# A Mamba-2 scan pipelined by one chunk, with three of its products on GpSimd

## The chip, the cores and the metric

One core of a Trainium2 chip runs the kernel. The metric is the device time of one execution in microseconds (us); less is better. TensorE (PE in the profile) multiplies matrices, VectorE (DVE) and ScalarE (ACT) work element by element, GpSimd (POOL) too, and SyncE (SP) issues most DMAs. Every engine works through its own queue in order.

## The reference

Two layers over 2048 tokens of width 1024, in float32: a Mamba-2 mixer, then multi-head latent attention, and a last norm. The change lies in the mixer's scan, which the reference computes in chunks:

```
def step(state, inp):
    x_c, dt_c, B_c, C_c = inp
    cum = jnp.cumsum(dt_c * A_g, axis=1)
    seg = cum[:, :, None] - cum[:, None, :]
    L = jnp.exp(jnp.where(causal, seg, -jnp.inf))
    CB = jnp.einsum('btgn,bsgn->btsg', C_c, B_c)
    y_intra = jnp.einsum('btsg,btsgh,bsgh,bsghp->btghp', CB, L, dt_c, x_c)
    y_inter = jnp.einsum('btgn,bghpn,btgh->btghp', C_c, state, jnp.exp(cum))
    w_end = jnp.exp(cum[:, -1:] - cum) * dt_c
    new_state = state * jnp.exp(cum[:, -1])[..., None, None] + \
        jnp.einsum('bsgn,bsgh,bsghp->bghpn', B_c, w_end, x_c)
    return new_state, y_intra + y_inter
```

There are 32 heads of width 64 in 4 groups; each group shares B and C of width 128. Around the scan stand an input projection (z, xBC and dt), a convolution of width 4 over xBC, a gate SiLU(z), a norm and an output projection.

## The kernel before

**Items.** `mamba` goes through 16 items: four blocks of 512 tokens (b), in each the four groups (g). An item's scan (`ssd`) works on four chunks of 128 tokens (c), so there are 64 chunks in all.

**What lies beside the scan.** `ssd` is a generator of 20 steps, five for each chunk. `mamba` runs other generators, the `parts`, and takes scan steps from `ssd` at even distances between their steps. The parts of item n are the output projection of item n-1 (`outp`, 8 steps), and for item n+1 the projection to xBC (`xbc`, 16 steps: a sweep for B and C, one for x) and to z (`zgate`, 8 steps). For items up to 4 the order is outp, xbc, zgate; after that xbc comes first. At every third group the next block's normalised x (`prep16`) and its time steps (`steps`) come last. So TensorE gets big products of 512 columns with the scan's small ones between them. The framework's scheduler makes each engine's queue from this order and the priorities; at run time the queues are in order.

**Big products.** A sweep fills up to four PSUM banks ("mm", four in all), three matmuls for each product (`mm3`, L403 to L405). A bank is emptied by `evacuate`: for xBC, GpSimd copies three halo columns into a tile `craw` (three buffers; L1055), ScalarE copies the bank behind them (L1056), GpSimd saves the new halo (L1057), ScalarE makes the first tap of the convolution (L1060), VectorE the other three (cacc, L1062) and after a Tanh the last product (L1065). For z it is one Tanh and one VectorE operation (sz, L1092), for the output one VectorE operation (hs, L1121).

**A chunk of the scan**, in its five steps (small results go to the PSUM tag "tr", four banks):

1. The cumulated log decays of eight heads are fetched by one DMA, broadcast to 128 partitions, into a tile "big" of 128x1024 (two buffers, L1225). TensorE transposes B and multiplies B with C; B and C are split into halves (high and low part) for products of three matmuls. ScalarE makes the decays: eight Relu with a bias (L1237) and one Exp (L1238). VectorE multiplies them by the masked CB (L1239).
2. TensorE transposes x (L1244). VectorE makes Xd, x times dt (L1247), and y, x times D (L1250). ScalarE makes Xw, x times wend, in eight operations of 64 columns (L1253); wend holds dt.
3. Xw is split into halves Xp: ScalarE copies the high one (L1208), GpSimd subtracts (L1209). Sixteen small matmul pairs of the decays and Xd (L1260) give the chunk's own part, which VectorE adds to y (L1261). From the second chunk on C times the state (halves Sp) is added, scaled by ecum (L1266, L1267).
4. B times Xp gives the state's increment (`late3`, L410 to L412, the low half of Xp last). VectorE multiplies the state by its decay (L1277) and adds (L1278); the new state is split into halves Sp (one buffer; ScalarE and GpSimd).
5. y is multiplied by the gate (L1283), scaled, split and transposed, for `outp` of the next item.

`steps` computes dt, its cumulated sums and exponentials for a block; its work tile is a "big" buffer. `out_power` finds a scale for the output weights once, at item 4.

## Time and profile before

| | |
|---|---|
| time, median of 3 runs (lowest to highest) | 2924.01 us (2920.55 to 2924.09) |
| the profiled execution | 2919.59 us; span of its instructions 2917.8 us |
| granted TensorE clock, mean | 0.993 |
| busy, share of the span | PE 2802.7 us (96%), DVE 2189.3 (75%), ACT 1854.4 (64%), POOL 985.2 (34%) |
| DMA | 507.56 MB, mean 174 GB/s |

The span is the time from the first to the last instruction. A row of a stage view gives for each engine the busy time and the number of instructions; a row of waits gives who waited for whom, the total in us, how many times and the longest; a row of a group gives line, engine, operation, output and inputs with their shapes, the count, the busy time and mean ns of one, and the idle time before them with what ended it. Busy times of TensorE are the union of pipelined matmuls, so short waits between them do not show as idle. L numbers are lines of the kernel before.

### The profile page before, as it was taken

The page shows a single profiled execution, that of the slowest core. Times are in us where ns is not written, and L with a number is a line of the kernel's source. Part 1 is how long each engine was busy: PE and PEld are TensorE (multiplying, and loading weights), DVE is VectorE, ACT ScalarE, POOL GpSimd, SP SyncE. Part 2 cuts the span into 40 slices and gives each one's busy share as a digit, 9 for nine tenths or more (in the row PEclk, how much of TensorE's full clock was granted, in tenths as well). Part 3 has the DMA queues.
Part 4 walks back from the last instruction along what each step waited for, and adds up shares of the span by engine and source line. Part 5 has one row for each costly group of instructions (what it writes and reads, how often), then busy time and mean ns, then how long its engine had stood idle before and what let it go on. Part 6 is the DMA issues. An engine that isn't in the chain of part 4 may idle for free.

```text
span 2917.8 us, 48835 instructions
## 1 busy us (share of the span) xinstructions
PE 2802.7 (96%) x16349; PEld 1648.5 (56%) x16349; DVE 2189.3 (75%) x4757; ACT 1854.4 (64%) x4731; POOL 985.2 (34%) x1200
## 2 busy tenths in 40 slices
PE   7999999998999999999999999999999999999898
PEld 6787755444444444444455455454555555555587
DVE  6778888888877777788776654544888898889476
ACT  7888777666666555666555343432888888888322
POOL 1211112212111221122111212222888888888400
PEclk9999999999999999999999999999999999999899
DMA  5343356665657544476544765556899999999884
GB/s 187 90 120 96 97 167 209 190 186 175 186 157 241 172 127 145 121 223 189 150 140 114 240 200 193 175 171 207 165 183 182 188 187 182 182 188 197 220 265 154
DMA packets 602144, 507.56 MB, mean 174 GB/s; under 512 B 413954, under 2 KB 455938, under 8 KB 601892
## 3 DMA queue, kind: packets, MB, share of 16 engines
q1 hardware_dynamic: 590020, 466.03, 61.3%
q0 software_dynamic: 11872, 38.41, 3.7%
q8 instruction: 128, 2.10, 0.3%
q14 instruction: 124, 1.02, 0.1%
HBM read 303.37 MB, written 104.47 MB: 140 GB/s over the span
## 4 chain that ended last, share of the span: by engine, by line
PE 64%; DVE 14%; ACT 7%; DMA 7%; issue 5%; POOL 2%; SPq 1%; ACTq 0%; POOLq 0%; DVEq 0%
PE mm L403 11%; PE mm L405 11%; PE mm L404 11%; PE tr L403 5%; PE tr L405 5%; PE tr L404 5%; PE mm L1758 4%; DVE cacc L1062 3%; DMA big<-cumT 2%; PE tr L1758 2%; PE mm L1731 2%; DMA wraw<-in_ssm_w_in_dram 2%; PE tr L1731 2%; PE tr L1260 2%; ACT big L1237 1%
## 5 line engine op out<-in xcount | busy, mean ns | idle before, releaser
L1723 POOL TENSOR_TENSOR HL<-Pr,HL 128x512 f16<-128x512 f32 x320 | 370.0, 1156 | 25.6
L403 PE MATMUL mm<-xT,wsp 128*128 128x512 f16 (+1 forms) x800 | 308.4, 385 | 7.4 <-DVE sz L1092 5.3
L404 PE MATMUL mm<-xT,wsp 128*128 128x512 f16 (+1 forms) x800 | 306.1, 383 | 0.0
L405 PE MATMUL mm<-xT,wsp 128*128 128x512 f16 (+1 forms) x800 | 305.2, 383 | 0.6 <-DVE wsp L434 0.5
L1209 POOL TENSOR_TENSOR Xp<-Xw,Xp 128x512 fp32r<-128x512 f32 x64 | 87.2, 1363 | 563.1 <-ACT Xp L1208 536.5
L403 PE MATMUL mm<-wsp,xT 128*128 128x512 f16 (+2 forms) x640 | 233.6, 366 | 1.9 <-ACT craw L1056 1.3
L404 PE MATMUL mm<-wsp,xT 128*128 128x512 f16 (+2 forms) x640 | 232.9, 364 | 1.0 <-DVE wsp L442 1.0
L1717 ACT ACTIVATE Pr<-tr,nm 128x512 f32<-128x512 f32 (+3 forms) x332 | 206.2, 626 | 41.8 <-DVE nm L1712 40.1
L405 PE MATMUL mm<-wsp,xT 128*128 128x512 f16 (+2 forms) x640 | 232.5, 364 | 0.0
L1062 DVE SCALAR_TENSOR_TENSOR cacc<-craw,pack,cacc 128x512 f32<-128x512 f32 x288 | 220.8, 785 | 11.9 <-ACT cacc L1060 10.2
L1722 POOL CAST HL<-Pr 128x512 f16<-128x512 f32 x320 | 195.0, 609 | 91.2 <-ACT Pr L1717 88.7
L1717 ACT ACTIVATE Pr<-mm,nm 128x512 f32<-128x512 f32 (+3 forms) x308 | 191.9, 628 | 44.5 <-DVE nm L1712 38.7
L1706 DVE TENSOR_REDUCE mx<-tr 128x1 f32<-128x512 f32 (+3 forms) x332 | 195.6, 602 | 28.3 <-PE tr L1682 25.9
L403 PE MATMUL mm<-wsp,yT 128*128 128x512 f16 (+1 forms) x512 | 199.4, 389 | 13.3 <-DVE hs L1121 7.2
L1237 ACT ACTIVATE big<-big,d_cum 128x128 f32<-128x128 f32 x512 | 169.8, 391 | 55.4 <-DMA big<-cumT 54.8
L1706 DVE TENSOR_REDUCE mx<-mm 128x1 f32<-128x512 f32 (+3 forms) x308 | 182.1, 604 | 27.6 <-PE mm L1682 20.6
L404 PE MATMUL mm<-wsp,yT 128*128 128x512 f16 (+1 forms) x512 | 197.7, 386 | 0.5 <-DVE wsp L442 0.5
L405 PE MATMUL mm<-wsp,yT 128*128 128x512 f16 (+1 forms) x512 | 197.4, 386 | 0.0
L405 PEld LDWEIGHTS <-xT 128*128 128x128 f16 (+1 forms) x1280 | 124.5, 97 | 117.2 <-issue 2.6
L403 PEld LDWEIGHTS <-xT 128*128 128x128 f16 (+1 forms) x1280 | 125.0, 98 | 106.1 <-issue 14.4
L1253 ACT ACTIVATE Xw<-tr,d_wend 128x64 f32<-128x64 f32 x512 | 111.7, 327 | 111.7 <-DVE y L1250 99.4
L404 PEld LDWEIGHTS <-xT 128*128 128x128 f16 (+1 forms) x1280 | 125.6, 98 | 96.1 <-issue 6.8
(504 smaller groups left out, 7562.3 us busy)
## 6 DMA issues: line engine op xcount, KB each, us to landing
wsp<-w_d SPq DMA_DIRECT2D x68, 512.0 KB, 4.0
wraw<-in_ssm_w_in_dram SPq DMA_DIRECT2D x128, 256.0 KB, 3.4
big<-cumT SPq DMA_DIRECT2D x64, 512.0 KB, 4.2
wraw<-in_ssm_w_out_dram SPq DMA_DIRECT2D x64, 256.0 KB, 3.3
w_d<-wsp SPq DMA_DIRECT2D x32, 512.0 KB, 3.5
wsp<-wo_d SPq DMA_DIRECT2D x32, 512.0 KB, 4.4
st<-w_d SPq DMA_DIRECT2D x56, 256.0 KB, 2.9
wsp<-wu_d SPq DMA_DIRECT2D x28, 512.0 KB, 3.8
```

The costliest lines, as they stand in the source:

```text
L403: mm(out, l_hi, r_hi, start=start, stop=False)
L404: mm(out, l_hi, r_lo, start=False, stop=False)
L405: mm(out, l_lo, r_hi, start=False, stop=stop)
L1062: nc.vector.scalar_tensor_tensor(acc, raw[:, k:k + TB], wk[k], acc, ALU.mult, ALU.add)
L1237: act(E[:, h, :], E[:, h, :], AF.Relu, bias=ncum[:, h0 + h:h0 + h + 1])
L1253: act(Xw[:, hc], px[:, hc], AF.Copy, scale=wend[:, h0 + h:h0 + h + 1])
L1706: v.tensor_reduce(m[:, at:at + 1], s, AX.X, ALU.max, negate=True)
L1717: nc.scalar.activation(tile("Pr", n, j, c)[:, :w], bank("S", n, j, c)[:, :w], AF.Exp, bias=moves[(4 * n + j) % len(moves)], accum_out=sums ...
L1722: nc.gpsimd.tensor_copy(u[:, 0], x)
L1723: nc.gpsimd.tensor_tensor(u[:, 1], x, u[:, 0], ALU.subtract)
L1731: nc.tensor.transpose(bank("T", n, k)[:, j * P:(j + 1) * P], tile("Pr", n, j, k // 4)[:, k % 4 * P:(k % 4 + 1) * P], self.ident)
L1758: nc.tensor.matmul(o, weights, half(n, k, low), start=start, stop=not left[n][at[0]])
```

## The change

The scan's chunk is cut into functions, and the first two steps of chunk c+1 run within chunk c, across the border from one item to the next as well:

- `fetch` (the DMA of the decays) for chunk c+2 stands behind the product of chunk c that frees the buffer. Before the first chunk two are fetched.
- `decays` (step 1 without the DMA) for chunk c+1 is the first step of chunk c, `inputs` (step 2, and the halves Xp) for chunk c+1 the fourth. Step 2 is now the product of the chunk alone, step 3 both C times the state and the update of the state.
- The product of decays and CB goes from VectorE to GpSimd, and so does the state's decay. Xw is made from Xd in one GpSimd operation instead of eight on ScalarE, and wend no longer holds dt.
- The work tile of `steps` is a craw buffer with four parts in place of six, dA and cT taking the places of e and q.
- `out_power` is taken behind `xbc` of its item's parts instead of ahead of it.
- The convolution's tiles are given back at the end of `ssd` instead of at its start.

The diff; the removed lines left out stand in the functions above:

```
--- before.py
+++ after.py
@@ -880,7 +880,7 @@
     def mamba(self, cp):
         nc = self.nc
         self.state = [None] * G
-        self.xn, self.xT, self.dtv, self.conv, self.sz, self.yT, self.rr, self.hs = {}, {}, {}, {}, {}, {}, {}, {}
+        self.xn, self.xT, self.dtv, self.conv, self.sz, self.yT, self.rr, self.hs, self.scan, self.fetched = ({} for _ in range(10))
         items = [(b, g) for b in range(NB) for g in range(G)]
         self.load_x(0, self.a["x"][0:TB])
         self.layer_constants(cp)
@@ -892,12 +892,12 @@
             if n:
                 parts.append(self.outp(*items[n - 1]))
                 total += 8
-            if n == G:
-                parts.append(self.out_power())
             if n + 1 < len(items):
                 parts += [self.xbc(*items[n + 1]), self.zgate(*items[n + 1])]
                 if n > G:
                     parts[0:2] = parts[1::-1]
+                elif n == G:
+                    parts.insert(2, self.out_power())
                 total += 24
             else:
                 parts.append(self.mla_gate(0, 0))
@@ -922,7 +922,7 @@
             elif b == NB - 2:
 
                 parts = [self.beside(parts, self.keep2({0: (0, 1, 2), 1: (3, 4, 5), 3: (6, 7)}[g]))]
-            scan, done, step = self.ssd(b, g), 0, 0
+            scan, done, step = self.ssd(b, g, items[n + 1] if n + 1 < len(items) else None), 0, 0
             for part in parts:
                 for _ in part:
                     step += 1
@@ -1135,7 +1135,7 @@
             for n in range(2):
                 nc.tensor.matmul(ps[0:2 * H, :], w[:, k].rearrange("p n h -> p (n h)"), xT[k][:, n, :],
                                  start=k + n == 0, stop=k + n == KD)
-        wk = self.t(self.sp, "big", [P, D], bufs=2)
+        wk = self.t(self.sp, "craw", [P, TB + 3], bufs=3)
         rt = self.t(self.sp, "yt", [2 * H, TB], bufs=2)
         nc.scalar.activation(rt, ps[0:2 * H, :], AF.Copy, scale=self.un[0:2 * H] if b else 1.0)
         ps = self.t(self.pp, "tr", [P, TB], bufs=4)
@@ -1143,7 +1143,8 @@
             nc.tensor.transpose(ps[:, c * 2 * H:(c + 1) * 2 * H], rt[:, c * P:(c + 1) * P],
                                 self.ident[0:2 * H, 0:2 * H])
         both = ps[:, 0:8 * H].rearrange("p (c n h) -> p c n h", c=4, n=2)
-        raw, e, q, p, dA, cT = (wk[:, n * P:n * P + P] for n in range(6))
+        raw, e, q, p = (wk[:, n * P:n * P + P] for n in range(4))
+        dA, cT = e, q
 
         def tmp(tag):
             return self.t(self.sp, tag, [P, P])
@@ -1182,38 +1183,93 @@
         nc.scalar.activation(dec, ps[:, P:2 * P], AF.Exp, scale=-1.0)
         v.tensor_tensor(wend, ps[:, P:2 * P], ncum, ALU.add)
         nc.scalar.activation(wend, wend, AF.Exp, scale=-1.0)
-        v.tensor_tensor(wend, wend, dt, ALU.mult)
         v.tensor_copy(cT, ps[:, 2 * P:3 * P])
         d = self.fd.tile([P, P], F32, name=self.name("cumT"), tag="cumT")
         nc.sync.dma_start(d, cT)
         self.dtv[b] = dt, ncum, ecum, dec, wend, d
         yield
 
-    def ssd(self, b, g):
+    def pair(self, tag, n, bufs):
+        return self.t(self.sp, tag, [P, 2, n], F32R, bufs=bufs)
+
+    def halves(self, u, x):
+        self.nc.scalar.activation(u[:, 0], x, AF.Copy)
+        self.nc.gpsimd.tensor_tensor(u[:, 1], x, u[:, 0].bitcast(F32), ALU.subtract)
+        return u
+
+    def fetch(self, b, g, c):
+
+        E = self.fetched[b, g, c] = self.t(self.sp, "big", [P, D], bufs=2).rearrange("p (h t) -> p h t", h=8)
+        h0, cumT = c * H + g * 8, self.dtv[b][5]
+        self.nc.sync.dma_start(E.rearrange("p h t -> p (h t)"),
+                               cumT[h0:h0 + 8, :].rearrange("h t -> (h t)").partition_broadcast(P))
+
+    def decays(self, b, g, c):
+
+        nc, act = self.nc, self.nc.scalar.activation
+        dt, ncum, ecum, dec, wend, cumT = self.dtv[b]
+        BT, CT = self.conv[b, g][0:2]
+        s, h0 = slice(c * P, (c + 1) * P), c * H + g * 8
+        E = self.fetched.pop((b, g, c))
+        pb = self.t(self.pp, "tr", [P, TB], bufs=4)
+        nc.tensor.transpose(pb[:, 0:P], BT[:, s], self.ident)
+        nc.tensor.matmul(pb[:, P:2 * P], BT[:, s], CT[:, s], start=True, stop=True)
+        Bt, Ct = self.pair("Bt", P, 2), None
+        self.split(Bt[:, 0], Bt[:, 1], pb[:, 0:P])
+        if b + c:
+            Ct = self.halves(self.pair("Ct", P, 2), CT[:, s])
+        CB = self.t(self.sp, "CB", [P, P], bufs=2)
+        nc.vector.tensor_tensor(CB, pb[:, P:2 * P], self.triu, ALU.mult)
+        for h in range(8):
+            act(E[:, h, :], E[:, h, :], AF.Relu, bias=ncum[:, h0 + h:h0 + h + 1])
+        act(E, E, AF.Exp, scale=-1.0)
+        nc.gpsimd.tensor_tensor(E, E, CB.unsqueeze(1).to_broadcast([P, 8, P]), ALU.mult)
+        self.scan[b, g, c] = [E, Bt, Ct]
+
+    def inputs(self, b, g, c):
 
         nc, v, act = self.nc, self.nc.vector, self.nc.scalar.activation
         dt, ncum, ecum, dec, wend, cumT = self.dtv[b]
-        BT, CT, *xs = self.conv.pop((b, g))
-        szs = self.sz.pop((b, g))
+        xs = self.conv[b, g][2:]
+        s, h0 = slice(c * P, (c + 1) * P), c * H + g * 8
+
+        def v8(x):
+            return x.rearrange("p (h d) -> p h d", h=8)
+
+        px = self.t(self.pp, "tr", [P, TB], bufs=4)
+        for j in range(4):
+            nc.tensor.transpose(px[:, j * P:(j + 1) * P], xs[j][:, s], self.ident)
+        Xd, Xw = self.t(self.sp, "Xd", [P, TB], bufs=2), self.t(self.sp, "Xw", [P, TB], bufs=1)
+        with self.tc.high_priority(20):
+            v.tensor_tensor(v8(Xd), v8(px), dt[:, h0:h0 + 8].unsqueeze(2).to_broadcast([P, 8, 64]), ALU.mult)
+        y = self.t(self.sp, "y", [P, TB], bufs=2)
+        skip = self.Dsk[:, g * 8:g * 8 + 8].unsqueeze(2).to_broadcast([P, 8, 64])
+        v.tensor_tensor(v8(y), v8(px), skip, ALU.mult)
+        nc.gpsimd.tensor_tensor(v8(Xw), v8(Xd), wend[:, h0:h0 + 8].unsqueeze(2).to_broadcast([P, 8, 64]), ALU.mult)
+        Xp = self.halves(self.pair("Xp", TB, 1), Xw)
+        self.scan[b, g, c] += [Xd, y, Xp]
+
+    def ssd(self, b, g, after):
+
+        nc, v, act = self.nc, self.nc.vector, self.nc.scalar.activation
+        dt, ncum, ecum, dec, wend, cumT = self.dtv[b]
         ms, e2 = self.t(self.sm, "ms", [P, 4]), self.t(self.sm, "e2y", [P, 4], I32)
         self.yT[b, g] = []
 
         def v8(x):
             return x.rearrange("p (h d) -> p h d", h=8)
 
...
+        if b + g == 0:
+            self.fetch(0, 0, 0)
+            self.fetch(0, 0, 1)
+            self.decays(0, 0, 0)
+            self.inputs(0, 0, 0)
+        szs = self.sz.pop((b, g))
         if b:
-            old = halves(pair("Sp", TB, 1), self.state[g])
+            old = self.halves(self.pair("Sp", TB, 1), self.state[g])
         for c in range(4):
-            s = slice(c * P, (c + 1) * P)
             h0 = c * H + g * 8
+            later = (b, g, c + 1) if c < 3 else after and (*after, 0)
 
             def heads(x):
                 return x[:, h0:h0 + 8].unsqueeze(2).to_broadcast([P, 8, 64])
@@ -1221,51 +1277,25 @@
             first = b == 0 and c == 0
             last = b == NB - 1 and c == 3
 
...
+            if later:
+                self.decays(*later)
             yield
...
+            E, Bt, Ct, Xd, y, Xp = self.scan.pop((b, g, c))
             yi = self.t(self.pp, "tr", [P, TB], bufs=4)
             for h in range(8):
                 hc = slice(h * 64, (h + 1) * 64)
                 for t in (slice(0, 64), slice(64, P)):
                     nc.tensor.matmul(yi[t, hc], E[:, h, t], Xd[:, hc], start=True, stop=True)
             v.tensor_tensor(y, y, yi, ALU.add)
+            if c < 2 or after:
+                self.fetch(*((b, g, c + 2) if c < 2 else (*after, c - 2)))
+            yield
             if not first:
                 pi = self.t(self.pp, "tr", [P, TB], bufs=4)
                 self.late3(pi, Ct[:, 0], Ct[:, 1], old[:, 0], old[:, 1])
                 t = self.t(self.sp, "yt", [P, TB], bufs=2)
                 v.tensor_tensor(v8(t), v8(pi), heads(ecum), ALU.mult)
                 v.tensor_tensor(y, y, t, ALU.add)
-            yield
             if not last:
                 pst = self.t(self.pp, "tr", [P, TB], bufs=4)
                 self.late3(pst, Bt[:, 0], Bt[:, 1], Xp[:, 0], Xp[:, 1])
@@ -1274,10 +1304,13 @@
                     v.tensor_copy(st, pst)
                 else:
                     st = self.state[g]
-                    v.tensor_tensor(v8(st), v8(st), heads(dec), ALU.mult)
+                    nc.gpsimd.tensor_tensor(v8(st), v8(st), heads(dec), ALU.mult)
                     v.tensor_tensor(st, st, pst, ALU.add)
                 if c < 3:
-                    old = halves(pair("Sp", TB, 1), st)
+                    old = self.halves(self.pair("Sp", TB, 1), st)
+            yield
+            if later:
+                self.inputs(*later)
             yield
             if b:
                 v.scalar_tensor_tensor(y, y, self.un, szs[c], ALU.mult, ALU.mult)
@@ -1314,6 +1347,7 @@
         else:
             v.tensor_scalar(rr, r, 0.5, None, ALU.mult)
         self.rr[b, g] = rr
+        del self.conv[b, g]
 
 
     def ev(self, dt=F16):
```

36 lines of the change are left out of this document (removed).

## The prediction

> **What bounds the kernel now.** I read the stages first: the busy time of each engine, stage by stage. The scan runs from 86 to 1580 us.
>
> ```profile
> core 0: us, PE busy (x) PEld busy (x) DVE busy (x) ACT busy (x) POOL busy (x), PEclk, DMA share, GB/s
> 86.00:390.00 304.00, 298.58 (x1718) 234.01 (x1718) 250.90 (x477) 248.48 (x666) 61.99 (x69) 1.00 0.37 110
> 390.00:765.00 375.00, 344.80 (x1988) 180.38 (x1987) 306.62 (x572) 254.46 (x590) 75.17 (x93) 0.98 0.60 186
> 765.00:1150.00 385.00, 362.86 (x2143) 182.81 (x2142) 293.69 (x625) 238.12 (x583) 71.45 (x96) 1.00 0.54 164
> 1150.00:1580.00 430.00, 414.26 (x2592) 216.55 (x2591) 334.63 (x731) 257.35 (x643) 84.54 (x106) 1.00 0.55 164
> ```
>
> TensorE is the bound, but it is not full: 5.4 + 30.2 + 22.1 + 15.7 = 73 us of the 1494 are idle. VectorE is next (1186 us, 79%), ScalarE has 998 us (67%), GpSimd only 293 us (20%). What this change can win lies in the 73 us. So the second view is who TensorE waited for in this stretch (total us, times, longest).
>
> ```profile
> PE tr L412 <- POOL Xp L1209: 13.6, 18, 1.4
> PE tr L1260 <- DVE big L1239: 10.1, 6, 2.2
> PE tr L1260 <- issue: 9.7, 7, 3.3
> PE mm L403 <- DVE hs L1121: 7.2, 4, 3.3
> PE mm L403 <- ACT craw L1056: 7.1, 9, 1.8
> PE tr L1260 <- DVE Xd L1247: 5.4, 4, 2.3
> PE mm L403 <- DVE sz L1092: 5.3, 5, 1.6
> ```
>
> Four rows are the scan's own chain within a chunk: the state product waits for the low half of Xp (13.6), and the product of a chunk (L1260) for its decays, "big" (10.1), or its inputs Xd (5.4). The row "issue" names no releaser, so I looked at its longest case in the timeline, VectorE and TensorE alone.
>
> ```profile
> 602.23 1.40 DVE L1062 SCALAR_TENSOR_TENSOR cacc<-craw,pack,cacc 128x512 f32<-128x512 f32 x2
> ...
> 603.55 0.68 DVE L1247 TENSOR_TENSOR Xd<-tr,d_dt 128x512 f32<-128x512 f32 x1
> ...
> 604.75 0.74 DVE L1062 SCALAR_TENSOR_TENSOR cacc<-craw,pack,cacc 128x512 f32<-128x512 f32 x1
> 605.41 1.22 DVE L1239 TENSOR_TENSOR big<-big,CB 128x1024 f32<-128x1024 f32 x1
> ...
> 606.73 0.55 PE L1260 MATMUL tr<-Xd,big 128*64 128x64 f32 x5 [3.27 <-issue]
> ```
>
> TensorE starts 0.1 us after the decay product ends (606.63), so "issue" is the decays too. They are late because VectorE works through the convolution (cacc) ahead of them. Together the four rows are 13.6 + 10.1 + 9.7 + 5.4 = 38.8 us. The other three rows (19.6 us) are PSUM banks of the big products that VectorE or ScalarE empties late.
>
> A long wait costs twice. Below are three more waits at L1260, from the timeline, and then four stretches that begin within 1 us of the end of these four waits; PEclk, third from the right, is the granted clock.
>
> ```profile
> 437.88 1.23 PE L1260 MATMUL tr<-Xd,big 128*64 128x64 f32 x32 [2.23 <-DVE big L1239]
> 905.72 1.40 PE L1260 MATMUL tr<-Xd,big 128*64 128x64 f32 x32 [2.13 <-DVE big L1239]
> 1285.76 1.97 PE L1260 MATMUL tr<-Xd,big 128*64 128x64 f32 x32 [2.48 <-issue]
> ```
>
> ```profile
> 438.80:442.30 3.50, 3.50 (x16) 1.67 (x13) 3.50 (x7) 2.98 (x11) 0.83 (x1) 0.51 0.53 181
> 606.10:613.00 6.90, 6.27 (x42) 3.74 (x43) 6.23 (x10) 3.77 (x13) 1.91 (x3) 0.51 0.23 76
> 906.40:909.90 3.50, 3.50 (x24) 1.95 (x20) 3.50 (x6) 3.13 (x11) 0.90 (x3) 0.51 0.61 228
> 1285.30:1288.80 3.50, 3.04 (x35) 2.65 (x35) 3.50 (x7) 1.75 (x8) 0.00 (x0) 0.51 0.35 120
> ```
>
> These 17.4 us at 0.51 lose 8.5 us.
>
> **The change part by part.**
>
> 1. *Decays and inputs a chunk ahead.* `decays` and `inputs` of chunk c+1 now run in steps 1 and 4 of chunk c, across the border of a group too. A chunk is 1494 / 64 = 23 us in five steps, so the decays get six steps to the product that reads them, Xd three and Xp four: 13 us at least, where the longest wait above is 3.3. All 38.8 us go, and the 8.5 us of slow clock with them: **-47.3**. Late next is what empties the banks (hs, sz, craw). The state's halves (Sp) had four steps to their reader and get five; TensorE waits for them in none of the rows.
>
> 2. *The fetch of the decays.* Its 64 DMAs stay 64, and each is issued two chunks ahead, right behind the product that frees its buffer.
>
> ```profile
> big<-cumT SPq DMA_DIRECT2D x64, 512.0 KB, 4.2
> ...
> SPq L1225 <- PE tr L1260: 40.0, 31, 3.7
> ...
> L1237 ACT ACTIVATE big<-big,d_cum 128x128 f32<-128x128 f32 x512 | 169.8, 391 | 55.4 <-DMA big<-cumT 54.8
> L1253 ACT ACTIVATE Xw<-tr,d_wend 128x64 f32<-128x64 f32 x512 | 111.7, 327 | 111.7 <-DVE y L1250 99.4 <-PE tr L1260 5.9 <-DVE rr L507 4.5
> ```
>
> ScalarE's 54.8 us of waiting for it end, since 4.2 us lie in four steps (18 us). SP waits for the product as it does now (40.0 us), with weights and the transposes of y behind it. No wait for weights' DMAs stands among TensorE's, so I cost this at nothing; without that cover each would cost up to 3.7 us.
>
> 3. *Scaled inputs on GpSimd in one step.* ScalarE loses 111.7 us (eight of 327 ns each chunk, pipelined), and its 99.4 us of waiting behind y go. TensorE waits for ScalarE only at craw, so this is no term, but a part of the better case below.
>
> 4. *Three products for GpSimd.*
>
> ```profile
> L1239 DVE TENSOR_TENSOR big<-big,CB 128x1024 f32<-128x1024 f32 x64 | 78.1, 1221 | 0.9
> L1277 DVE TENSOR_TENSOR st<-st,d_dec 128x512 f32<-128x512 f32 x56 | 40.7, 727 | 42.0 <-POOL Sp L1209 41.9
> L1620 POOL TENSOR_TENSOR K<-wr,K x4: 2329/2578/2787, 2717.8 to 2737.4; 128x1024 fp32r<-128x1024 f32 x4
> L1209 POOL TENSOR_TENSOR Xp<-Xw,Xp 128x512 fp32r<-128x512 f32 x64 | 87.2, 1363 | 563.1 <-ACT Xp L1208 536.5 <-PE tr L1260 15.7 <-PE mm L405 10.0
> L1209 POOL TENSOR_TENSOR Sp<-st,Sp 128x512 fp32r<-128x512 f32 x60 | 83.2, 1386 | 165.9 <-ACT Sp L1208 160.0 <-PE mm L405 5.5
> L1209 POOL TENSOR_TENSOR Ct<-BC,Ct 128x128 fp32r<-128x128 f32 x60 | 37.8, 631 | 119.4 <-ACT Ct L1208 119.3
> ```
>
> VectorE loses 78.1 + 40.7 = 119 us. GpSimd gains 64 products of 128x1024, 2.33 to 2.79 us each by the nearest row (I take 2.4), and 56 + 64 of 128x512 at 1.36: 154 + 163 = 317 us, so some 610 of 1494 (41%). It does not become the bound. But its operations cost VectorE time:
>
> ```profile
> L1267 DVE TENSOR_TENSOR y<-y,yt 128x512 f32<-128x512 f32 x60 | 57.1, 952 | 1.0
> L1261 DVE TENSOR_TENSOR y<-y,tr 128x512 f32<-128x512 f32 x64 | 43.8, 684 | 51.8 <-PE tr L1260 51.7
> L1062 DVE SCALAR_TENSOR_TENSOR cacc<-craw,pack,cacc x288: 728/747/1786, 37.2 to 1465.1; 128x512 f32<-128x512 f32 x144
> L1062 DVE SCALAR_TENSOR_TENSOR cacc<-craw,pack,cacc 128x512 f32<-128x512 f32 x288 | 220.8, 785 | 11.9 <-ACT cacc L1060 10.2
> L1267 DVE TENSOR_TENSOR y<-y,yt x60: 677/691/1796, 105.9 to 1562.4; 128x512 f32<-128x512 f32 x60
> ```
>
> The sum from two SBUF tiles takes 952 ns, with one operand in PSUM 684: 60 x 0.268 = 16 us. cacc has a median of 747 and a mean of 785: 288 x 0.038 = 11 us. That is 27 us of stretch beside 208 us of GpSimd's subtractions (87.2 + 83.2 + 37.8), 0.13 per us; with the smaller forms I take 0.2. The added 317 us then stretch VectorE by 63 us, and VectorE still ends 56 us lower. TensorE: nothing. Bounds: none at all, or as in the lock rival.
>
> The Trainium skill's page "SBUF — State Buffer", section "Who interferes with whom", calls the ports that both engines share an exclusive lock: a VectorE instruction with two SBUF inputs and a GpSimd instruction that reads SBUF exclude each other for a whole instruction. The longest y above (1796 for 691) agrees, the cacc mean hardly does. If some such instruction always stood waiting, the added 317 us would hold VectorE for half of each, an estimate of 158 us, and VectorE would end 39 us higher instead of 56 lower.
>
> 5. *GpSimd's queue.* The decay product waits there for ScalarE's exponential. Behind it stand the halo copies of the convolution, which ScalarE's next step of the convolution (L1060) and so the next bank wait for.
>
> ```profile
> L1055 POOL COPY craw<-halo x96: 185/577/3028, 1.1 to 1457.9; 128x3 f32<-128x3 f32 x96
> ```
>
> They already take 577 ns in the median, 185 at best, and up to 3028. The products hold GpSimd for 154 / 1494 = 10% of the time: of 96 copies ten meet one, at 1.2 us each: **+12**, if all of it reaches TensorE. Bounds: 0, and 77 us (the slower rival).
>
> 6. *Small moves.* The work tile of `steps` goes from a decay buffer to a craw buffer; its steps come last in their group, and the convolution that needs craw a product sweep later. `out_power` moves behind its item's xBC products. Both at nothing; without the cover each costs a wait of the craw kind, below 1.8 us, a few times.
>
> Sum: -47 + 12 = **-35**. The profiled execution took 2919.6 us (span 2917.8, 1.8 around it); it becomes 2885. The median of the three runs is 2924.0, 4.4 higher, and I forecast on that scale: **2889**.
>
> **The rivals.**
>
> *Better.* VectorE 56 us and ScalarE 112 us lighter also empty the banks in time, and the halo copies cost nothing: -47 - 20 = -67, so 2857. For it: what VectorE does late stands behind cacc, as in the timeline. Against: nothing that shortens cacc is in the change. A part of it is likelier: 2866.
>
> *The lock.* A decay product holds back a VectorE instruction for 1.2 us in the mean, 64 times, and a third of these 77 us comes at a bank that TensorE waits for (an assumption): -35 + 26 = -9, 2915. For it: the rows of 1786 and 1796. Against: 0.13 per us as measured.
>
> *Handed on.* VectorE runs late at 602 to 606 whatever it works on; the waits at L1260 return as waits for hs and sz, and only Xp's 13.6 is won: -14 + 12, 2922.
>
> *Slower: halo copies behind the decay products.* Sixteen groups have two convolution sweeps each. If a decay product stands ahead in each of the 32 and delays it by its whole 2.4 us, 77 us come back against 47: +30, 2954. It turns into a loss from 1.5 us a sweep on. For it: the 3028 ns copy, and one queue in order. Against: of 23 us per chunk GpSimd holds 9.5.
>
> *The change does not do what it says:* the fetch waits for its buffer until the decays are due. The SP row's longest wait, 3.7 us, is far below 18, so I give it nothing of its own.
>
> **How the numbers follow.** This kernel's measurement can tell 0.2%, 5.8 us. Forecast (2872 to 2908) 0.53; better 0.17; lock (2905 to 2925) 0.13, of which 0.06 faster, 0.05 the same, 0.02 slower; handed on 0.06, the same; slower 0.11. So faster 0.76, same 0.11, slower 0.13. The range leaves out the slower rival and the best end of the better one: 2860 to 2930.
>
> **What would show it.** Step 1: no waits at L1260 for big, Xd or issue, and none of L412 for Xp; PEclk 1.00 between 390 and 1580. Step 2: ScalarE's wait for big's DMA gone. Step 4: decay products of 2.4 us on GpSimd, cacc's mean below 830. Step 5: craw waits near today's 7 us plus 12. The prediction is wrong if hs, sz and craw together pass 60 us, if GpSimd is over 60% busy in the scan, or if the products on GpSimd with broadcast operands take over 4 us.

## The result, and the profile after

The changed kernel takes 2966.4 us (median of 4 runs, 2964.7 to 2968.8) against 2924.1 us before on the same chip: 1.0146 times as long, 95% interval 1.0129 to 1.0164. It is slower by 42 us where 35 less were forecast.

The stages of the kernel after. The scan now ends near 1630 us instead of 1580; the later stages have kept their lengths to 2 us.

```profile
core 0: us, PE busy (x) PEld busy (x) DVE busy (x) ACT busy (x) POOL busy (x), PEclk, DMA share, GB/s
86.00:390.00 304.00, 287.74 (x1611) 227.07 (x1610) 244.67 (x428) 224.95 (x550) 118.81 (x102) 0.98 0.33 101
390.00:765.00 375.00, 335.31 (x1912) 177.64 (x1911) 301.14 (x508) 224.08 (x465) 151.25 (x135) 0.96 0.56 174
765.00:1150.00 385.00, 359.51 (x2129) 184.25 (x2127) 284.34 (x577) 208.43 (x444) 148.00 (x144) 0.98 0.56 171
1150.00:1630.00 480.00, 455.80 (x2823) 241.48 (x2822) 352.29 (x771) 242.35 (x517) 174.68 (x167) 0.98 0.53 159
```

TensorE's idle time in the scan rose from 73 us to 16.3 + 39.7 + 25.5 + 24.2 = 106, and the granted clock of the whole span fell from 0.993 to 0.984, which is 0.007 x 2918 = 20 us lost before and 0.016 x 2965 = 47 now. Idle time and lost clock together grew by 33 + 27 = 60 us and the span by 47; that the other 13 us are slow clock in idle time is likely, but was not measured apart. Whom TensorE waits for, 86 to 1640 us:

```profile
PE mm L403 <- ACT craw L1056: 33.8, 28, 5.4
PE mm L403 <- DVE hs L1121: 14.6, 13, 2.8
PE mm L403 <- DVE sz L1092: 12.2, 6, 3.2
PE tr L1336 <- DVE y L1318: 10.7, 5, 3.5
...
PE tr L1288 <- POOL big L1226: 1.9, 1, 1.9
```

The scan's four rows of before (38.8 us) are gone but for one wait of 1.9 us. The three rows of banks that are emptied late (hs, sz and craw, the tiles into which VectorE and ScalarE empty them) have grown from 19.6 us to 60.6. A row of the scan that was small has come up as well: in the first block TensorE transposes y itself (L1336), and it waits 10.7 us for y, against 0.4 us for the same row before. The longest case in the timeline, ScalarE, GpSimd and TensorE, and the window behind it:

```profile
1310.94 1.13 ACT L713 ACTIVATE wraw<-hx,pack 128x1024 bf16<-128x1024 f32 x1
...
1312.83 1.04 POOL L1248 TENSOR_TENSOR Xw<-Xd,d_wend 128x512 f32<-128x512 f32 x1
...
1313.91 0.63 ACT L1196 ACTIVATE Xp<-Xw 128x512 fp32r<-128x512 f32 x1 [1.74 <-POOL Xw L1248]
...
1316.28 0.67 ACT L1056 ACTIVATE craw<-mm,un 128x512 f32<-128x512 f32 x1
...
1317.00 0.59 PE L403 MATMUL mm<-wsp,yT 128*128 128x512 f16 x1 [5.36 <-ACT craw L1056]
```

```profile
1316.50:1323.50 7.00, 6.50 (x20) 2.79 (x20) 6.86 (x14) 6.53 (x11) 1.87 (x6) 0.57 0.84 258
```

Behind other work, ScalarE has a wait for GpSimd's Xw in its queue ahead of the bank's copy (craw). TensorE stands 5.36 us and then runs at a clock of 0.57 for 7 us.

The engines' busy time, from the page, and then groups of VectorE and GpSimd, both over all of the span:

```profile
PE 2818.1 (95%) x16349; PEld 1662.8 (56%) x16349; DVE 2183.0 (74%) x4633; ACT 1752.6 (59%) x4219; POOL 1286.3 (43%) x1384
```

```profile
L1062 DVE SCALAR_TENSOR_TENSOR cacc<-craw,pack,cacc 128x512 f32<-128x512 f32 x288 | 243.4, 869 | 19.1 <-ACT cacc L1060 17.0 <-POOL craw L1055 0.8
L1226 POOL TENSOR_TENSOR big<-big,CB 128x1024 f32<-128x1024 f32 x64 | 163.6, 2556 | 264.2 <-DVE CB L1222 228.7 <-DVE rsy L789 7.5 <-issue 6.8
L1248 POOL TENSOR_TENSOR Xw<-Xd,d_wend 128x512 f32<-128x512 f32 x64 | 72.2, 1128 | 67.9 <-DVE Xd L1244 67.7
L1307 POOL TENSOR_TENSOR st<-st,d_dec 128x512 f32<-128x512 f32 x56 | 68.1, 1216 | 3.4
```

119 us of products left VectorE, and its busy time fell from 2189.3 only to 2183.0: everything else on it became 112 us longer. cacc went from 785 to 869 ns in the mean. Not every operation became longer. The first two lines below are hs and one of the weights' operations (wsp) before, the next two the same after; the operation on hs reads a PSUM bank, the one on wsp reads its tiles from SBUF:

```profile
L1121 DVE SCALAR_TENSOR_TENSOR hs<-mm,rr,hs 128x512 f32<-128x512 f32 x128 | 92.5, 744 | 11.9 <-PE mm L405 11.8
L442 DVE SCALAR_TENSOR_TENSOR wsp<-wraw,rw,wsp 128x512 f16<-128x512 f32 x64 | 48.9, 781 | 13.6 <-ACT wsp L441 13.6
...
L1121 DVE SCALAR_TENSOR_TENSOR hs<-mm,rr,hs 128x512 f32<-128x512 f32 x128 | 91.9, 741 | 9.1 <-PE mm L405 8.6
L442 DVE SCALAR_TENSOR_TENSOR wsp<-wraw,rw,wsp 128x512 f16<-128x512 f32 x64 | 61.4, 973 | 21.3 <-ACT wsp L441 21.3
```

Last, the waits of ScalarE and SyncE, 0 to 1640 us:

```profile
ACT big L1224 <- DMA big<-cumT: 113.1, 39, 11.1
ACT Xp L1196 <- POOL Xw L1248: 90.1, 57, 4.8
SPq L1204 <- PE tr L1288: 65.5, 35, 9.8
```

The decays are fetched two chunks ahead, yet ScalarE waits for them twice as long as before (54.8 us).

### The profile page after: what moved, and what is told of

It is laid out like the page before. It is cut to its first block, busy times and chain, and to the rows that moved or that the text cites. A ratio compares the mean times of both kernels' runs of the same rounds, so it can differ in the third digit from the quotient of the medians.

```text
span 2964.9 us, 48375 instructions
## 1 busy us (share of the span) xinstructions
PE 2818.1 (95%) x16349; PEld 1662.8 (56%) x16349; DVE 2183.0 (74%) x4633; ACT 1752.6 (59%) x4219; POOL 1286.3 (43%) x1384
## 4 chain that ended last, share of the span: by engine, by line
PE 62%; DVE 17%; ACT 7%; DMA 6%; issue 3%; POOL 3%; SPq 1%; ACTq 0%; DVEq 0%; POOLq 0%
PE mm L403 11%; PE mm L404 10%; PE mm L405 10%; PE tr L403 5%; PE tr L405 5%; PE tr L404 5%; PE mm L1792 4%; DVE cacc L1062 4%; DMA big<-cumT 2%; PE tr L1792 2%; PE mm L1765 2%; PE tr L1765 2%; DVE wsp L442 2%; DMA wraw<-in_ssm_w_in_dram 2%; DMA wraw<-in_ssm_w_out_dram 1%
## 5 line engine op out<-in xcount | busy, mean ns | idle before, releaser
L403 PE MATMUL mm<-xT,wsp 128*128 128x512 f16 (+1 forms) x800 | 313.2, 392 | 24.3 <-ACT craw L1056 9.2
L405 PE MATMUL mm<-xT,wsp 128*128 128x512 f16 (+1 forms) x800 | 309.9, 387 | 3.5 <-DVE wsp L434 1.7
L404 PE MATMUL mm<-xT,wsp 128*128 128x512 f16 (+1 forms) x800 | 309.1, 386 | 0.0
L1226 POOL TENSOR_TENSOR big<-big,CB 128x1024 f32<-128x1024 f32 x64 | 163.6, 2556 | 264.2 <-DVE CB L1222 228.7
L1062 DVE SCALAR_TENSOR_TENSOR cacc<-craw,pack,cacc 128x512 f32<-128x512 f32 x288 | 243.4, 869 | 19.1 <-ACT cacc L1060 17.0
L403 PE MATMUL mm<-wsp,xT 128*128 128x512 f16 (+2 forms) x640 | 236.4, 370 | 13.9 <-DVE hs L1121 6.1
L1224 ACT ACTIVATE big<-big,d_cum 128x128 f32<-128x128 f32 x512 | 163.9, 388 | 135.1 <-DMA big<-cumT 113.1
L404 PE MATMUL mm<-wsp,xT 128*128 128x512 f16 (+2 forms) x640 | 235.0, 367 | 1.8 <-DVE wsp L442 1.8
L405 PE MATMUL mm<-wsp,xT 128*128 128x512 f16 (+2 forms) x640 | 234.8, 367 | 0.0
L404 PE MATMUL mm<-wsp,yT 128*128 128x512 f16 (+1 forms) x512 | 199.8, 390 | 0.9 <-DVE wsp L442 0.9
L404 PEld LDWEIGHTS <-xT 128*128 128x128 f16 (+1 forms) x1280 | 125.8, 98 | 106.4 <-issue 19.1
L1197 POOL TENSOR_TENSOR Sp<-st,Sp 128x512 fp32r<-128x512 f32 x60 | 88.9, 1481 | 180.1 <-ACT Sp L1196 180.1
```

The source lines that it names most:

```text
L403: mm(out, l_hi, r_hi, start=start, stop=False)
L404: mm(out, l_hi, r_lo, start=False, stop=False)
L405: mm(out, l_lo, r_hi, start=False, stop=stop)
L1062: nc.vector.scalar_tensor_tensor(acc, raw[:, k:k + TB], wk[k], acc, ALU.mult, ALU.add)
L1224: act(E[:, h, :], E[:, h, :], AF.Relu, bias=ncum[:, h0 + h:h0 + h + 1])
L1226: nc.gpsimd.tensor_tensor(E, E, CB.unsqueeze(1).to_broadcast([P, 8, P]), ALU.mult)
```

## The experiments

Each is told with its difference to the kernel before or after; the ratio is to the kernel before on the same chip. That kernel's median lies between 2921.1 and 2925.8 us on the chips used, so a difference of less than 5 us between experiments on different chips says nothing. "Pipelined kernel" means the change with its three products back on their old engines.

**The parts alone.** e1, the pipelined kernel:

```
-        nc.gpsimd.tensor_tensor(E, E, CB..., ALU.mult)      # decays
+        nc.vector.tensor_tensor(E, E, CB..., ALU.mult)
-        nc.gpsimd.tensor_tensor(v8(Xw), v8(Xd), wend..., ALU.mult)
+        for h in range(8): act(Xw[:, hc], px[:, hc], AF.Copy, scale=wend[...])
-                    nc.gpsimd.tensor_tensor(v8(st), v8(st), heads(dec), ALU.mult)
+                    v.tensor_tensor(v8(st), v8(st), heads(dec), ALU.mult)
```

> The changed kernel (2966 us), with its three products put back where they were: decays times CB and the state's decay on VectorE, Xw in eight operations on ScalarE, wend with dt. What is left of the change is the pipelining by a chunk, the early fetch and the small moves. Three theories of the loss. Theory A (ScalarE stands behind GpSimd: in the changed kernel ScalarE waits 90 us for Xw, with the bank copies craw behind it): faster than before, about 2890, craw waits of TensorE back near 7 us. Theory B (GpSimd's products hold VectorE at the shared ports): also about 2890, cacc's mean back at 785 ns. Theory C (the fetch lands late: ScalarE waits 113 us for the decays' DMA, 54.8 before, with craw behind it): stays slow, about 2955, the 113 us stay.

2932.2 us, 1.0032 (1.0021 to 1.0042).

e2, the kernel before with the three products on GpSimd and nothing else:

> The kernel before (2924 us) with only its three products moved to GpSimd (decays times CB, state's decay, Xw from Xd in one operation), nothing pipelined. Theory A: slower, about 2960, ScalarE waits some 90 us for Xw. Theory B: slower, about 2960, cacc's mean near 870 ns, ScalarE's wait for Xw small beside it. Theory C: near 2924 plus what the longer decay product (2.56 us for 1.22) adds ahead of TensorE's L1260, 64 times up to 1.3 us: 2924 to 3000, and the wait for the decays' DMA stays at 55 us.

2991.2 us, 1.0228 (1.0211 to 1.0245). e3, the kernel before with the two small moves alone (the work tile of `steps`, the place of `out_power`):

> The kernel before with only the two small moves: the work tile of the time steps in a craw buffer, and out_power behind xBC. All theories: 2924 within 6 us. If it moves by more, the order of the queues, which the scheduler makes anew for every edit, is worth that much by itself, and smaller differences between the other kernels say nothing.

2913.3 us, 0.9967 (0.9954 to 0.9980). Both large halves lose, and the small moves that the prediction had at nothing win 11 us. That is more than the 6 us named beforehand, and the expectation says what follows: the scheduler makes the queues anew for every edit, and a difference of about this size can come from that alone. The account below rests on differences of 19 us and more; those of 5 to 12 us are rough sizes. From e3 to e1, pipelining costs 19 us; from e1 to the whole change, the products cost 34. In e2 nothing is pipelined, so the longer decay product stands in the chunk's own chain as well, and its 67 us are not a price of GpSimd's load alone.

**Which product?** e4 is the change with Xw back on ScalarE, e6 with the decays' product back on VectorE.

> The changed kernel with Xw alone put back on ScalarE (eight operations from PSUM, wend with dt); decays times CB and the state's decay stay on GpSimd, the pipelining stays. Theory A: the loss goes, 2900 or lower, ScalarE's 90 us of waiting for Xw are gone, craw waits below 12 us. Theory B: GpSimd loses 72 of its added 304 us, so a quarter of the loss comes back: about 2955. Theory C: about 2960, 113 us of waiting for the decays' DMA stay.

> The changed kernel with only the product of decays and CB back on VectorE; Xw and the state's decay stay on GpSimd. Theory A: about 2955, since GpSimd gets to Xw earlier but ScalarE still waits for it. Theory B: GpSimd loses 164 of its added 304 us, cacc's mean falls from 877 towards 820 ns, and half of the loss comes back: about 2945. Theory C (fetch): 2960.

e4: 2941.4 us, 1.0057 (1.0042 to 1.0072). e6: 2931.4 us, 1.0026 (1.0014 to 1.0038). The prices do not add. The decays' product costs 35 us on top of the other two (whole change less e6), but with the state's decay and without Xw the two cost 9 (e4 less e1). Xw costs 25 on top of the other two (whole change less e4), but with the state's decay and without the decays' product the two cost nothing (e6 less e1, -1). VectorE's cacc in e4 and then in e6, over the whole span, and a wait of ScalarE in e6, 86 to 1640 us:

```profile
L1062 DVE SCALAR_TENSOR_TENSOR cacc<-craw,pack,cacc 128x512 f32<-128x512 f32 x288 | 240.8, 855 | 44.5 <-ACT cacc L1060 42.4 <-POOL craw L1055 0.3
L1062 DVE SCALAR_TENSOR_TENSOR cacc<-craw,pack,cacc 128x512 f32<-128x512 f32 x288 | 221.5, 793 | 17.1 <-ACT cacc L1060 14.8 <-POOL craw L1055 0.3
```

```profile
ACT Xp L1196 <- POOL Xw L1248: 84.9, 54, 4.3
```

In e1 cacc takes 787 ns. So it is the decays' product that stretches cacc; Xw and the state's decay alone leave it where it was. But the stretch is not the whole price: e4 has most of it (855 of the change's 869 ns) and stands only 9 us above e1.

**Is it ScalarE's wait for Xw (90.1 us)?** e5 lets GpSimd copy the high half of Xp too, so that ScalarE has no business with Xw:

```
-        Xp = self.halves(self.pair("Xp", TB, 1), Xw)
+        Xp = self.pair("Xp", TB, 1)
+        nc.gpsimd.tensor_copy(Xp[:, 0], Xw)
+        nc.gpsimd.tensor_tensor(Xp[:, 1], Xw, Xp[:, 0].bitcast(F32), ALU.subtract)
```

> The changed kernel (2966 us) with the high half of Xp copied by GpSimd too, so that ScalarE waits for GpSimd at no Xp; GpSimd's load only grows (64 copies). Theory A (ScalarE's queue stands behind GpSimd's Xw, worth the 25 us between the changed kernel and the one with Xw on ScalarE): 2940 or lower, ScalarE's 90 us of waiting for Xw gone, craw waits of TensorE from 33.8 to below 20. Theory B (the load of GpSimd at the shared ports and in its queue): 2966 or slower.

2968.7 us, 1.0156 (1.0141 to 1.0171): no gain. The edit also gives GpSimd 64 more copies that read SBUF, and cacc's mean goes from 877 to 917 ns (86 to 1600 us), so e5 alone can't tell whether the wait was harmless or whether the copies ate what its end won:

```profile
L1062 DVE SCALAR_TENSOR_TENSOR cacc<-craw,pack,cacc 128x512 f32<-128x512 f32 x270 | 240.7, 917 | 8.6 <-ACT cacc L1060 6.8 <-POOL craw L1055 0.6
```

e6 says more: there ScalarE waits 84.9 us for Xw, and the time is e1's. So that wait, the plain reading of the timeline above, costs no more there than the lighter ScalarE and VectorE win. Whether it costs something beside the decays' product, where Xw is worth 25 us, stays open.

**Is it load on GpSimd as such?** e8 adds four products of 128x256 in each chunk, from constants, whose result nobody reads, to the kernel before.

> The kernel before (2924 us) with four products of 128x256 more for each chunk on GpSimd, from constants into a tile that nothing reads: some 2.7 us a chunk, 175 us of load, that no engine waits for by data. Theory B: VectorE's instructions with two SBUF inputs stretch (cacc's mean from 788 to 830 ns) and the halo copies come later: 2935 to 2945. Theory A: within 6 us of 2924, since ScalarE waits for nothing new.

3037.5 us, 1.0398 (1.0381 to 1.0414). They depended on nothing, so all 256 ran within the first 212 us, and single waits of TensorE reached 50.1 us: it shows a blocked queue, and is no measure of the load. e12 ties the load to the chunk by reading CB, which every chunk makes:

```
+            scratch = self.t(self.sp, "scratch", [P, 256], F16, bufs=1)
+            for _ in range(4):
+                nc.gpsimd.tensor_tensor(<scratch as 2 x 128>, <CB, twice>, <pack as 2 x 128>, ALU.mult)
```

> The kernel before with GpSimd's load as in the last such run (four products of 128x256 for each chunk, 2.7 us, read by nothing), but each reading the chunk's CB, so that they come once a chunk and not in bursts. Theory B, load alone (the shared ports and GpSimd's queue): 2935 to 2950, cacc's mean above 830 ns. If it is within 6 us of 2924, 2.7 us of GpSimd a chunk cost nothing by themselves, and the loss needs a consumer that waits for them.

2968.6 us, 1.0140 (1.0124 to 1.0157). e14 puts a load at the same place of the queue that hardly reads: one column's product of CB, and eight memsets of the scratch tile.

> The kernel before with a load on GpSimd as in the run behind CB, but of eight memsets of 128x256 for each chunk and one product of one column that reads CB: GpSimd reads nearly nothing of SBUF and stands in its queue for CB all the same. Theory ports: cacc's mean stays at 788 ns, within 8 us of 2924. Theory queue (what comes behind the load on GpSimd waits: halo copies, Xp and Sp halves): 2945 or slower, with waits of TensorE for Xp above 25 us.

2928.9 us, 1.0014 (1.0003 to 1.0024). The groups of e12 (a product and cacc) and then those of e14, over the whole span:

```profile
L1238 POOL TENSOR_TENSOR scratch<-CB,pack 128x256 f16<-128x256 f32 x256 | 279.1, 1090 | 395.6 <-DVE CB L1235 353.0
...
L1062 DVE SCALAR_TENSOR_TENSOR cacc<-craw,pack,cacc 128x512 f32<-128x512 f32 x288 | 229.9, 817 | 11.2 <-ACT cacc L1060 9.6
```

```profile
L1237 POOL TENSOR_TENSOR scratch<-CB,pack 128x1 f16<-128x1 f32 x64 | 53.7, 838 | 369.4 <-DVE CB L1235 343.5
...
L1239 POOL MEMSET scratch<- 128x256 f16 x512 | 161.5, 315 | 28.7
L1062 DVE SCALAR_TENSOR_TENSOR cacc<-craw,pack,cacc 128x512 f32<-128x512 f32 x288 | 219.1, 779 | 11.6 <-ACT cacc L1060 9.8
```

279 us of products that read SBUF, consumed by nobody, cost 43 us; 215 us of work that mostly writes cost 4. A chunk's batch holds the queue for 4 x 1.09 = 4.4 us in e12 and 0.84 + 8 x 0.315 = 3.4 us in e14, so a halo copy behind it waits 1 us less in e14, at most; standing in the queue for 3.4 us a chunk costs little. The engines' busy time in e12 and then in e14:

```profile
PE 2816.9 (95%) x16349; PEld 1653.3 (56%) x16349; DVE 2239.5 (75%) x4757; ACT 1855.9 (63%) x4731; POOL 1260.9 (42%) x1456
```

```profile
PE 2807.4 (96%) x16349; PEld 1649.3 (56%) x16349; DVE 2195.3 (75%) x4757; ACT 1854.8 (63%) x4731; POOL 1197.9 (41%) x1776
```

VectorE's rose by 50 us in e12 and 6 in e14. Two things remain mixed in: a product is also longer than a memset, and e12 holds the queue for 1 us a chunk more.

**Why does pipelining lose?** e7 is the pipelined kernel with no fetch: the Relus read a constant tile (values of the decays left out). e11 does the same to the kernel before.

```
-        E = self.fetched.pop((b, g, c))
+        E = self.t(self.sp, "big", [P, D], bufs=2)...
-            act(E[:, h, :], E[:, h, :], AF.Relu, bias=...)
+            act(E[:, h, :], self.ones, AF.Relu, bias=...)
```

> The pipelining alone (2932 us), with the fetch left out: the decays are computed from a constant tile in place of the fetched sums, with the same instructions on every engine, so the output is not the reference's. Theory C (in the pipelined kernels ScalarE stands 110 to 125 us at the decays' DMA, with craw behind it): 2905 or lower, craw waits from 22.8 to below 10. Rival (handed on: TensorE, freed of the scan's waits, meets banks that VectorE and ScalarE empty as late as ever): within 8 us of 2932, the waits for craw, hs and sz stay at 45 us.

> The kernel before (2924 us) with the fetch left out, the decays computed from a constant tile in the same instructions (so the output is not the reference's). It tells what the pipelining is worth where no fetch is late. Theory C: ScalarE's 55 us of waiting go, 2905 to 2915, so that the pipelining alone without a fetch (2883) stands 20 to 30 us lower: the scan's waits that were predicted. Rival (the pipelining is worth nothing): 2883 as well.

e7: 2883.0 us, 0.9863 (0.9849 to 0.9878). e11: 2905.6 us, 0.9931 (0.9913 to 0.9949). So the fetch costs 19 us in the order of before and 49 in the pipelined one. Without it, pipelining and the small moves win 23 us together; if the moves keep their 11, pipelining is worth about 12. TensorE's waits in e1 and then in e7, 86 to 1600 us:

```profile
PE mm L403 <- ACT craw L1056: 22.8, 22, 3.0
PE mm L403 <- DVE hs L1121: 13.4, 11, 1.9
PE mm L403 <- DVE sz L1092: 9.3, 7, 3.0
PE mm L404 <- DVE wsp L442: 8.5, 3, 7.4
PE mm L403 <- ACT xT L441: 7.0, 2, 5.9
```

```profile
PE mm L403 <- DVE hs L1121: 12.2, 10, 1.6
PE mm L403 <- ACT craw L1056: 12.2, 17, 2.4
PE mm L403 <- DVE sz L1092: 4.3, 4, 2.0
PE mm L404 <- DVE wsp L442: 2.6, 2, 2.2
```

With the fetch TensorE waits more for banks (craw, sz) and for weights and inputs in their float16 halves (wsp, xT), which ScalarE and VectorE make. Where ScalarE stands is in e1's timeline, TensorE and ScalarE:

```profile
958.89 1.15 PE L1291 MATMUL tr<-Xd,big 128*64 128x64 f32 x32
...
965.50 1.28 ACT L1225 ACTIVATE big<-big,d_cum 128x128 f32<-128x128 f32 x4 [1.67 <-DMA big<-cumT]
```

The product that frees the buffer ends at 960.04, and the Relus that read the new fetch begin at 965.50 after a wait: not four steps later, but as soon as the transfer lands. The scheduler has put them so early into ScalarE's queue that they stand waiting for it, ahead of two copies of banks (at 971.17 and 973.57 in the same timeline).

e9 gives the pipelined kernel a third buffer and fetches one chunk earlier (Xd with one buffer, Xw in a cacc buffer, for the room); e10 does it to the whole change.

```
-        ... self.t(self.sp, "big", [P, D], bufs=2)
+        ... self.t(self.sp, "big", [P, D], bufs=3)
-            if c < 2 or after:
-                self.fetch(*((b, g, c + 2) if c < 2 else (*after, c - 2)))
+            if c < 1 or after:
+                self.fetch(*((b, g, c + 3) if c < 1 else (*after, c - 1)))
```

> The pipelining alone (2932 us) with three decay buffers in place of two, and the fetch one chunk earlier: behind the product of chunk c stands the fetch for chunk c+3. The room comes from Xd (one buffer in place of two) and Xw (in a buffer of the convolution's cacc). Theory C (the fetch, 2932 against 2883 without it): ScalarE's wait for the decays' DMA falls from 125 to below 30 us, and the time to 2885 to 2905. Rival (not the wait, but the DMA's traffic or the constant tile made the kernel without a fetch fast): 2925 or slower, whatever ScalarE's wait.

> The whole changed kernel (2966 us) with the same three buffers and the earlier fetch. If the fetch and GpSimd's load add up: about 2966 - 40 = 2925. If GpSimd's load is the bound by itself once the fetch is early: 2950 or more, with craw waits of TensorE still above 20 us.

e9: 2922.7 us, 0.9992 (0.9980 to 1.0003). e10: 2968.6 us, 1.0146 (1.0127 to 1.0165). The group of Relus in e9 (86 to 1600 us) waits for the transfer as much as in e1 (125.1 us):

```profile
L1225 ACT ACTIVATE big<-big,d_cum 128x128 f32<-128x128 f32 x488 | 156.8, 390 | 133.2 <-DMA big<-cumT 128.2 <-PE tr L411 4.8
```

So the number of buffers is not what makes it wait; the Relus must have moved forward with the fetch. e13 holds them back: in ScalarE's queue they may only come behind the last operation on the previous chunk's y. e15 does it to the whole change.

```
+        with self.tc.issue_after(self.squared) if self.squared else nullcontext():
             for h in range(8):
                 act(E[:, h, :], E[:, h, :], AF.Relu, bias=...)
...
-            act(junk, y, AF.Square, ...)
+            self.squared = act(junk, y, AF.Square, ...).ins
```

> The pipelining alone (2932 us, two buffers), with the Relus of the next chunk queued on ScalarE behind the Square of the previous chunk's y, where the fetch has long landed. Theory D (the Relus stand in ScalarE's queue directly behind the fetch, which takes 4.5 us and more, so that the craw copies behind them wait): ScalarE's wait for the decays' DMA falls from 125 to below 40 us, craw waits below 15, time 2890 to 2910. Rival (the transfer itself is late, or the waits move to the decays): the wait stays, or TensorE waits at the chunk's product again, 2925 or slower.

> The whole changed kernel (2966 us) with the Relus held back in the same way. If the two losses are independent: 2966 less what the same edit brings to the pipelining alone, some 2930. If GpSimd's load takes it all: above 2955, since the product of decays and CB on GpSimd then starts later and Xw, Xp and the halo copies stand behind it.

e13: 2924.8 us, 0.9995 (0.9983 to 1.0007). e15: 2987.7 us, 1.0216 (1.0191 to 1.0240). The Relus of e13 and then three waits of its TensorE, 86 to 1600 us:

```profile
L1227 ACT ACTIVATE big<-big,d_cum 128x128 f32<-128x128 f32 x496 | 166.9, 410 | 0.3 <-DMA big<-cumT 0.3
```

```profile
PE mm L404 <- DVE wsp L442: 10.5, 6, 3.6
PE mm L403 <- ACT craw L1057: 10.4, 11, 2.2
PE mm L403 <- DVE sz L1093: 4.7, 6, 2.0
```

The 125 us are gone, and the waits for banks are back at the height of e7; yet it saves 7 us of the 49 only, and the rows of the weights stay (wsp on L404 is at 2.6 us in e7). SyncE's wait for the product that frees the buffer did not fall: it is 40.0 us before, 74.4 in e1 and 97.1 in e13. In the whole change, holding the Relus loses 21 us more; why was not traced.

Is it the transfer or the waiting around it? e16 lets the pipelined kernel fetch into a tile that nobody reads, with the decays from a constant tile; e17 is its control without the fetch, in the same layout.

```
-        E = self.fetched[b, g, c] = self.t(self.sp, "big", [P, D], bufs=2)...
+        E = self.t(self.sp, "far", [P, D], bufs=1)...
```

> The pipelined kernel with the products on their old engines, its 64 fetches issued as they are but into a tile that nobody reads; the decays come from a constant tile, so that neither SyncE waits for the product nor ScalarE for the transfer (values of the decays left out; to make room Xd has one buffer and Xw lies in a cacc buffer, as in the control beside it). If it is the waiting around the fetch that eats the pipelining's gain, the time is within 8 us of the control. If it is the transfer itself (32 MB beside the weights, DMA issue slots), it is 25 us or more above the control, near 2915 to 2925.

> Control: the same layout with no fetch at all (values of the decays left out). Expected 2880 to 2890, like the pipelined kernel without the fetch (2883), if the one buffer of Xd and the place of Xw cost nothing.

e16: 2901.4 us, 0.9916 (0.9897 to 0.9935). e17: 2882.6 us, 0.9847 (0.9832 to 0.9863). The fetch that nobody waits for costs 19 us. It is not only the transfer, though: with nothing to wait for the fetches came in bursts, far ahead (the group of issues below, with their count and the first and the last start), and SyncE stood behind one for the next (its waits, 86 to 1600 us).

```profile
L1205 SPq DMA_DIRECT2D far<-cumT x64: 319/326/890, 43.2 to 1213.9; - x64
```

```profile
SPq L1205 <- DMA far<-cumT: 123.9, 42, 6.3
```

Whether these 19 us are the transfer's or SyncE's stays open. It speaks for the other 30 of the 49 us lying in the waiting, without showing it: SyncE's for the product that frees the buffer, with weights behind it in its queue, and the Relus' for the transfer. e13 puts 7 of them on the latter; the former was not tried alone.

**Which small move?** e18 has the work tile of `steps` in a craw buffer alone.

> The kernel before with the work tile of steps in a convolution buffer alone. If this edit makes the 11 us that the two small moves win together, about 2913; if the move of out_power makes them, 2924.

2920.1 us, 0.9982 (0.9972 to 0.9993): about 5 of the 11 us. The rest falls to `out_power` by difference; it was not run alone, and why either wins was not traced.

Of the runs that keep the decays' values none beat e3, which is faster than both kernels.

## Why the prediction was wrong, step by step

Two steps failed by what they put at nothing: step 2, where the runs show about 30 us for the fetch, and the part "TensorE: nothing" of step 4, where they show 34 us for the products. Step 1 was about four times too large. One of the prediction's own signs of being wrong came true, narrowly: hs, sz and craw together are at 60.6 us.

*Step 1 (decays and inputs ahead), -47.* The mechanism is right: the four rows are gone. The size is wrong. With no fetch in the way, pipelining is worth about 12 us (e11 against e7, less the small moves, if these keep their worth there). The step took a wait that is removed for time that is won; in e7 craw, hs and sz are already at 12.2 + 12.2 + 4.3 = 28.7 us against 19.6 before. The rival "handed on" had this mechanism, but only for hs and sz and with 0.06.

*Step 2 (the fetch), nothing.* This step failed. "4.2 us lie in four steps" took the place of a line in the program for its place in the queue. The Relus sit where the transfer lands, ScalarE's wait rose from 54.8 to 113.1 us instead of ending, SyncE's wait for the product from 40.0 to 65.5 instead of staying, and the fetch costs 49 us in the pipelined order against 19 before: 30 us that the sum did not have. The step also looked for trouble at one place, the weights' DMAs among TensorE's waits. It came one link further on, at wsp and xT, which ScalarE and VectorE make from what these DMAs bring. The rival that the fetch "waits for its buffer until the decays are due" did not see this either: the third buffer left ScalarE's wait as it was.

*Step 3 (Xw).* ScalarE became 102 us lighter (1854.4 to 1752.6), and it helped nobody: it now waits 90 us for Xw. Alone with the state's decay the move costs nothing (e6), on top of the decays' product 25 us (e4).

*Step 4 (products on GpSimd), VectorE -56 and TensorE nothing.* The durations were right (2.56 us for 2.4, 1.13 and 1.22 for 1.36), as was GpSimd's share (593 of 1544 us, 38%, for 41%). The stretch was mis-sized: 112 us beside 304 us of new products, 0.37 per us for the assumed 0.2 (129 us and 0.42 against e1, which differs in the products alone), and cacc at 869 ns, above the 830 named. So VectorE became no lighter: it ends 6 us below the kernel before and 10 us above e1 (2173.3 us). And "TensorE: nothing" failed: the change costs 34 us over e1. VectorE's balance does not explain that by itself, since in e4 it is 14 us below e1 (2159.7) and the kernel still 9 us slower. As the rows of lines and waits read, the added time falls on operations like cacc and the weights' halves, while hs and sz keep their length (744 and 741 ns, 683 and 680) and come late behind them. That this makes the 34 us is argued from e12 and e14, not shown for the change; why Xw adds 25 us to the decays' product is open.

The Trainium skill's page "SBUF — State Buffer", section "Who interferes with whom", states that a VectorE instruction with two SBUF inputs contends with a GpSimd instruction that reads SBUF, and not with one that only writes it. The pair e12 and e14 agrees: 43 us against 4. The size lies between: a full lock was put at 158 us of stretch in the prediction, 112 to 129 were measured, and the unread products of e12 give 50 beside 279 us. The lock rival named the decays' product, which e4 and e6 bear out. Its 26 us lie between the 9 that this product costs with the state's decay alone (e4) and the 35 that it costs on top of both others (e6); its time was off because it started from a sum of -35.

*Step 5 (halo copies), +12.* No run shows this term. In the change ScalarE waits for the halo copies in no row and VectorE for 0.8 us, and a copy takes 578 ns in the median as before. The slower rival's 2954 us came nearest to the time, for the wrong reason: e14 holds the same queue for 3.4 us a chunk and costs 4 us, and TensorE's wait for GpSimd's own work is 1.9 us.

*Step 6 (small moves), nothing.* They win 11 us, about 5 of them by the work tile of `steps`; the term of step 5 was as large, and this one was taken for nothing.

Together: -11 for the small moves, +19 for pipelining with its fetch (-12 and +30, to 1 us), +34 for the products, is +42, the measured difference. That it adds up follows from taking differences along one chain of kernels; the second and third parts depend on each other (e6, e15), and another order would give other parts.

## What to carry to other kernels

On an engine that is a full queue, count for each removed wait what stands next in that queue; here 39 us of waits went, which won about 12 us without the fetch, and cost 19 with it. Before trusting that a load is "a chunk ahead", look in the timeline for where the scheduler puts its first reader: here, without an order of its own, the reader stood waiting for the transfer in a queue that others needed. Holding it back is only part of the cure (e13). An idle GpSimd is not free room beside a busy VectorE: price a product moved there by what it adds to VectorE's operations with two inputs in SBUF, not by GpSimd's own busy share, and try the products one by one: here two of the three cost nothing without the third.

## What the runs showed of the hardware

GpSimd products that read SBUF lengthen VectorE's work by 0.18 us (e12) to 0.37 us (the change) for each us they run, while memsets of GpSimd leave cacc at 779 ns against 785 before. hs and sz, which read a PSUM bank, keep their length beside the change's products. cacc is at 817 ns beside products of 1.09 us (e12), at 793 beside Xw and the state's decay (1.13 and 1.19 us, e6), and at 855 with the decays' product in Xw's place (2.52 us, e4); whether its length or its place in time makes the difference was not tried.

TensorE's clock fell to 0.57 over the 7 us behind a single wait of 5.36 us, and to 0.51 behind the waits of 2.1 to 3.3 us that the prediction quotes. The Trainium skill's page "TensorE: Matmul & The Clock Gate", section "What's actually happening", names an idle window of about 3.4 us, free-running, as the condition for the half clock. The 5.36 us agree; the shorter waits before show that the clock also falls where no wait alone is that long.
